# Fifteen copies of x issued on SyncE instead of GpSimd, and a conditional block in place of a zero-or-one loop

## The chip, the core and the metric

One NeuronCore of a Trainium2 chip runs the whole program. The metric is the device time of one execution in microseconds, as the median of several. All engine times below come from one profiled execution; a line such as L678 is line 678 of the kernel before.

## What is computed

Two transformer blocks for one sequence of 512 tokens of width 1024, in float32. The first has an SSD (Mamba-2) mixer beside a forgetting attention of 16 heads, and a convolution-gated MLP. The second has retention, sliding-window attention, a two-level mixture of 32 experts with two experts for each token, and a gated per-layer embedding. What the change touches:

```python
# first block, forgetting attention (x itself is not needed for it)
logits = einsum(qh, kh) * scale + cum[..., None] - cum[:, :, None, :]
# second block, experts: top-1 group, then top-2 experts inside it
combine = sum(one_hot(expert_id) * (g_w * top_p)[..., None])
for grp in range(4):
    hid = silu(einsum('td,edf->tef', hf, w_gate[sl])) * einsum('td,edf->tef', hf, w_up[sl])
    y = y + einsum('tef,efd->td', hid * combine[:, sl, None], w_down[sl])
x = x + y
x = x + sigmoid(rms_norm(x, ple_gate_norm_g) @ w_ple_gate) * ple
```

## The kernel before, in words

Each float32 product is made of three passes over a high and a low part (`mm3`, L251 to L253), so TensorE carries nearly the whole program. Weights come in chunks of 128x1024 through `fetch` (L217), which issues a 512 KB transfer on SyncE into a `wr` tile; ScalarE makes the high part `wh` (L205) and VectorE or GpSimd the low part `wl` (L208). In the first block there are two `wr` tiles and three pairs of `wh` and `wl`, so a transfer waits for a free `wr`, and a split for a free pair.

The stages follow one another: load x and the constants and normalise x (L361 to L363) tile by tile, with `n_mix`, one row of weights spread over all partitions (L351); the projection z (L416); the gates and their sums, written to the DRAM tile `sums` (L476); the SSD mixer in two groups (L480 to L582), which reads `sums` back into `ab` (L546); the forgetting attention for four groups of heads, two pairs of heads each, which reads `sums` back into `ncum` (L680); and then the other stages up to the experts and the closing gate with the output (`gated`, L1858 to L1861).

`ydram` is a DRAM tile of 30 x 64 rows of 1024 for the rows that the experts give. Before any expert writes to it, it is filled with rows of x: fifteen copies of 128 rows, 512 KB each, from DRAM to DRAM, so that rows that no expert writes hold finite numbers. They stand in the attention's loop in the code (L677, L678) and are issued by GpSimd. The experts' results are scattered into `ydram` by GpSimd near the end of the program (L1540) and gathered from it (L1796).

`overflow` (L1149) handles tokens beyond the 64 slots of an expert. Every engine loads two registers, `rounds` and `some` (L1157, L1159). `some` is 0 or 1, and the work stands in a loop over range(0, some) (L1161). In these inputs no expert has more than 64 tokens, so the body is not executed: the trace holds no instruction of it.

Nothing here but the stretches under `manual_schedule` has its order written by hand: the framework's list scheduler orders each engine's instructions, and puts an instruction with no open dependency as early as its queue allows. `tc.issue_after(ins)` adds an edge of issue order alone: what is traced inside the block on the engine of `ins` comes behind `ins` in that engine's queue. SyncE's queue is in order, and its transfers take turns on eight semaphores, so that a transfer also waits for the one eight places earlier to land.

Of the kernel before, what the change touches and what calls it, by code (L numbers as in the profile page):

```python
# [19 lines left out]
T = 512  # L20
# [384 lines left out]
def first_mixer(c, xt, zraws):  # L405

    tc, nc, a = c.tc, c.nc, c.a
# [58 lines left out]
    sums = c.dram.tile([2, 16, T], F32, name="sums")  # L466
# [123 lines left out]
    with tc.tile_pool(name="fox", bufs=1) as p:  # L590
        offs = [0, 128, 384, 768]

        def scores(qs, kd, kl, ncum):

            pb = p.tile([128, 1280], F32, name=c.name("pb"), tag="pb", bufs=2)
            den = c.sm([128, NT], tag="den")
            rden = c.sm([128, NT], tag="rden")
            for t in range(NT):
                n = 128 * (t + 1)
                tb = slice(t * 128, t * 128 + 128)  # L600
                sc = c.aux()
                pe.matmul(sc[:, :n], qs[:, tb], kd[:, :n], start=True, stop=False)
                pe.matmul(sc[:, :n], qs[:, tb], kl[:, :n], start=False, stop=False)
                pe.matmul(sc[:, tb], c.identb, c.upneg, start=False, stop=True)


                ns = p.tile([128, T], F32, name=c.name("ns"), tag="ns", bufs=3)
                nm = c.sm([128, 1], tag="nm", bufs=4)
                v.tensor_tensor_reduce(ns[:, :n], sc[:, :n], ncum[:, :n], scale=-1.0, scalar=3e38,
                                       op0=OP.add, op1=OP.min, accum_out=nm)  # L610
                pt_ = pb[:, offs[t]:offs[t] + n]
                s.activation(pt_, ns[:, :n], AF.Exp, scale=-1.0, bias=nm, accum_out=den[:, t:t + 1])
                v.reciprocal(rden[:, t:t + 1], den[:, t:t + 1])
                v.tensor_scalar(pt_, pt_, rden[:, t:t + 1], None, op0=OP.mult)
            return pb

        def values(pb, vv, out):

            po = c.aux()
            ptile = [p.tile([128, 1280], F32R, name=c.name("pT"), tag=f"pT{k}", bufs=2) for k in range(2)]  # L620
            pos = 0
            for js in ((0,), (1,), (2, 3)):
                pt = c.aux()
                o, spans = 0, []
                for j in js:
                    st = o
                    for t in range(j, NT):
                        c.transpose(pt[:, o:o + 128], pb[:, offs[t] + j * 128:offs[t] + j * 128 + 128])
                        o += 128
                    spans.append((j, pos + st, o - st))  # L630
                c.split(ptile[0][:, pos:pos + o], ptile[1][:, pos:pos + o], pt[:, :o])
                pos += o
                for j, st, n in spans:
                    for k in range(2):
                        pe.matmul(po[:, j * 128:], vv[:, j].rearrange("p x d -> p (x d)"),  # L635
                                  ptile[k][:, st:st + n], start=j == 0 and k == 0, stop=j == NT - 1 and k == 1)
            tmp = p.tile([64, T], F32, name=c.name("ot"), tag="ot", bufs=1)
            s.activation(tmp, po[64:128], AF.Copy)
            v.tensor_tensor(out, po[0:64], tmp, op=OP.add)


        kls = [[p.tile([128, T], F32R, name=c.name("kl")) for _ in range(n)] for n in (1, 2)]
        for i in range(2):
            for kl in kls[i]:
                v.memset(kl[64 - 64 * i:128 - 64 * i].bitcast(F32), 0.0)
        pending = []

        c.ydram = c.dram.tile([COMBINED * SLOTS, D], F32, name="ydram")
        blocks = [(i, a["x"][i % T:i % T + 128]) for i in range(0, COMBINED * SLOTS, 128)]
        for hg in range(4):  # L650
            qk = []
            for i in range(2):
                r = fin.tile([128, NT, 4, 64], F32, name=c.name("qk"), tag=f"qk{i}", bufs=2)
                ss = c.sm([128, NT, 4], tag="qss")

                def eat(tp, ps):
                    ps4 = ps.rearrange("p t (h d) -> p t h d", h=4)
                    sq = fin.tile([128, 2, 4, 64], F32, name=c.name("sq"), tag="sq", bufs=1)
                    s.activation(sq, ps4, AF.Square)
                    s.activation(r[:, 2 * tp:2 * tp + 2], ps4, AF.Copy)  # L660
                    v.tensor_reduce(ss[:, 2 * tp:2 * tp + 2], sq, axis=AX.X, op=OP.add)

                c.proj_b(xt, a["wqkv"][hg, i], eat)
                rs = c.rsqrt(ss.rearrange("p t h -> p (t h)"), 1.0 / 64, "qr")
                r3 = r.rearrange("p t h d -> p (t h) d")
                v.tensor_tensor(r3, r3, rs[:, :, None].to_broadcast([128, 16, 64]), op=OP.mult)
                qk.append(r)
            vv = fin.tile([128, NT, 4, 2, 64], F32R, name=c.name("v"), tag="v", bufs=2)

            def eat_v(tp, ps):  # L670
                ps4 = ps.rearrange("p t (h d) -> p t h d", h=4)
                t2 = slice(2 * tp, 2 * tp + 2)
                c.split(vv[:, t2, :, 0], vv[:, t2, :, 1], ps4)

            c.proj_b(xt, a["wqkv"][hg, 2], eat_v)
            for pr in range(2):
                for i, rows in blocks[4 * hg + 2 * pr:4 * hg + 2 * pr + 2]:  # L677
                    nc.gpsimd.dma_start(c.ydram[i:i + 128], rows)  # L678
                ncum = fin.tile([128, 2, T], F32, name=c.name("ncum"), tag="ncum", bufs=2)
                nc.sync.dma_start(ncum, sums[1, 4 * hg + 2 * pr:4 * hg + 2 * pr + 2][None].to_broadcast([128, 2, T]))  # L680
                pq, pk = c.aux(), c.aux()
                for ps, src in ((pq, qk[0]), (pk, qk[1])):
                    for t in range(NT):
                        c.transpose(ps[:, t * 128:t * 128 + 128],
                                    src[:, t, 2 * pr:2 * pr + 2].rearrange("p h d -> p (h d)"))

                qs = [p.tile([128, T], F32R, name=c.name("qs"), tag=f"qs{i}", bufs=2) for i in range(2)]
                kd = [p.tile([128, T], F32R, name=c.name("kd"), tag=f"kd{i}", bufs=2) for i in range(2)]
                kl = [k[pr % len(k)] for k in kls]
                kn = c.col("kn")  # L690
                for i in range(2):
                    hi, lo = slice(64 * i, 64 * i + 64), slice(64 - 64 * i, 128 - 64 * i)
                    s.activation(qs[i][hi], pq[hi], AF.Copy, scale=qn[hi])
                    v.scalar_tensor_tensor(qs[i][lo], pq[hi], qn[hi], qs[i][hi].bitcast(F32), op0=OP.mult, op1=OP.subtract)
                    s.activation(kd[i][hi], pk[hi], AF.Copy, scale=kn[hi])
                    s.activation(kd[i][lo], pk[hi], AF.Copy, scale=kn[hi])
                    v.scalar_tensor_tensor(kl[i][hi], pk[hi], kn[hi], kd[i][hi].bitcast(F32), op0=OP.mult, op1=OP.subtract)
                for i in range(2):
                    pb = scores(qs[i], kd[i], kl[i], ncum[:, i])
                    pending.append((pb, vv[:, :, 2 * pr + i], mixf[64 * i:64 * i + 64, 2 * hg + pr, :]))  # L700
                    if len(pending) > 1:
                        values(*pending.pop(0))
        for x in pending:
            values(*x)
# [444 lines left out]
def overflow(c, x, routing, slot, wt, extra, pled, out):  # L1149
# [3 lines left out]
    tc, nc, a = c.tc, c.nc, c.a  # L1153
# [4 lines left out]
                            skip_runtime_bounds_check_because="the count of tokens bounds it")  # L1158
    some = nc.values_load(extra[0:1, 1:2], min_val=0, max_val=1, skip_runtime_bounds_check_because="0 or 1")  # L1159
    wgu, wdn = a["wgu"].rearrange("e p c -> (e p) c"), a["wdn"].rearrange("e p c -> (e p) c")  # L1160
    with tc.For_i(0, some, 1):  # L1161
        ring = c.more_ring(2, 5)
        p = tc.alloc_tile_pool(name="over", bufs=1)
        rel = p.tile([128, 2, NT], F32, name="rel")
# [293 lines left out]
def experts(c, x, routing, xtp, pled, out):  # L1458
# [342 lines left out]
    for pool in (ring4, p, p0, ring3, op):  # L1801
        pool.release()
    routing.ring.release()
    overflow(c, x, routing, slot, wt, extra, pled, out)
    moe.release()

# [57 lines left out]
def emit(tc, a, out, dbg=None, stop=None):  # L1864
    with ExitStack() as ctx:
# [15 lines left out]
        for t in range(NT):  # L1881
            xn = c.sm([128, D], tag="xn", bufs=2, pool=x0)
            c.normalize(xin[t], w, xn, xn)
            c.to_xt(xn, _block(xt, t))
        x0.release()
        mixs, mixf, xpool, mixf_pool = first_mixer(c, xt, raws)
        xt = _xt_tiles(c, xtp, "xt")
        for t in range(NT):
# [43 lines left out]
```

## Time and profile before

| | |
|---|---|
| median of 3 runs (lowest to highest) | 1603.81 us (1602.76 to 1604.42) |
| the profiled execution: its own time | 1600.57 us |
| the profiled execution: span from the first to the last instruction | 1598.8 us |
| outside the span, in the profiled execution | 1.77 us |
| TensorE busy | 1517.5 us, 95% of the span |
| copies into ydram (L678) | 15 of 512 KB, 9.9 / 12.9 / 15.5 us from issue to landing (least / median / most) |

How to read it: the span is what the trace covers. PE is TensorE, PEld its weight loads, DVE VectorE, ACT ScalarE, POOL GpSimd, SP SyncE; a "q" behind a name (SPq, POOLq) marks what the engine's sequencer does alone, such as issuing a transfer, a wait or a branch. q0 is the queue of GpSimd's transfers, q1 that of SyncE's.

### The profile page before, as it was taken

To read this page: it belongs to the slowest core of one execution; us is meant where nothing else is said; L and a number is where in the kernel's file an instruction comes from. 1 tells how busy PE (TensorE), PEld (TensorE's weight loads), DVE (VectorE), ACT (ScalarE), POOL (GpSimd) and SP (SyncE) were. 2 spreads that over 40 slices of the span, in tenths; PEclk is the share of its full clock that TensorE was granted. 3 is DMA by queue.
4 is the path that set the end of the run, shared out by engine and by line. 5 is a ranking of instruction groups with operands and counts; after the bars stand their busy time and mean duration, and the time that the engine had idled before them with its cause. 6 is when DMAs were issued, how large, how long until landed. Compare 5 with 4: busy or idle time off the path is not lost.

```text
span 1598.8 us, 24250 instructions
## 1 busy us (share of the span) xinstructions
PE 1517.5 (95%) x9603; PEld 1254.7 (78%) x9603; DVE 898.8 (56%) x1980; ACT 663.1 (41%) x1103; POOL 111.2 (7%) x102
## 2 busy tenths in 40 slices
PE   4997999999999999999999999899999999999987
PEld 3776888998899988998889998787888864554456
DVE  4378778778874766336653523868654453223165
ACT  3364747567742544224442333569612421111133
POOL 3043310000000000000000000300000001000020
PEclk9998999999999999999999999999999999999999
DMA  9342222222341533233332433221323699999971
GB/s 321 94 157 80 66 67 80 93 79 68 106 145 41 169 96 98 74 106 106 97 92 90 163 105 102 93 93 48 98 66 126 242 338 410 409 410 410 402 275 56
DMA packets 75944, 246.62 MB, mean 154 GB/s; under 512 B 9486, under 2 KB 18446, under 8 KB 75456
## 3 DMA queue, kind: packets, MB, share of 16 engines
q1 hardware_dynamic: 69152, 220.80, 39.6%
q0 software_dynamic: 4944, 17.91, 3.0%
q10 hardware_dynamic: 1728, 6.29, 1.0%
q8 instruction: 78, 1.28, 0.3%
q14 instruction: 42, 0.34, 0.1%
HBM read 234.86 MB, written 24.18 MB: 162 GB/s over the span
## 4 chain that ended last, share of the span: by engine, by line
PE 74%; DVE 12%; ACT 6%; DMA 5%; issue 2%; POOL 0%; SPq 0%; ACTq 0%; DVEq 0%; POOLq 0%
PE acc L252 18%; PE acc L251 18%; PE acc L253 18%; PE acc L1117 5%; PE aux L355 3%; PE aux L1485 3%; PE acc L1137 3%; DMA wc<-in_wgu_dram 2%; DVE wl L208 1%; PE aux L635 1%; ACT wh L205 1%; DMA wr<-in_wz_dram 1%; PE aux L522 1%; DMA wc<-in_wpleg_dram 1%; DMA wc<-in_wdn_dram 1%
## 5 line engine op out<-in xcount | busy, mean ns | idle before, releaser
L208 DVE TENSOR_TENSOR wl<-wr,wh 128x1024 fp32r<-128x1024 f32 (+1 forms) x177 | 213.7, 1210 | 266.0 <-ACT wh L205 260.9
L205 ACT ACTIVATE wh<-wr 128x1024 fp32r<-128x1024 f32 (+1 forms) x181 | 188.4, 1046 | 328.7 <-PE acc L253 166.9
L253 PE MATMUL acc<-xth,wl 128*128 128x512 f32 (+2 forms) x744 | 278.1, 374 | 0.1
L252 PE MATMUL acc<-xtl,wh 128*128 128x512 f32 (+2 forms) x744 | 277.9, 374 | 0.0
L251 PE MATMUL acc<-xth,wh 128*128 128x512 f32 (+2 forms) x744 | 277.8, 373 | 0.1
L251 PE MATMUL acc<-wh,xth 128*128 128x256 f32 x912 | 257.3, 283 | 4.4 <-ACT xth L205 2.2
L252 PE MATMUL acc<-wl,xth 128*128 128x256 f32 x912 | 256.8, 282 | 2.1 <-DVE wl L208 2.1
L253 PE MATMUL acc<-wh,xtl 128*128 128x256 f32 x912 | 256.8, 283 | 0.8 <-DVE xtl L208 0.8
L251 PEld LDWEIGHTS acc<-wh,xth 128*128 128x128 f32 x912 | 172.1, 189 | 7.1 <-ACT xth L205 2.8
L252 PEld LDWEIGHTS acc<-wl,xth 128*128 128x128 f32 x912 | 172.2, 189 | 4.5 <-DVE wl L208 3.4
L253 PEld LDWEIGHTS acc<-wh,xtl 128*128 128x128 f32 x912 | 172.1, 189 | 1.6 <-DVE xtl L208 1.0
L251 PEld LDWEIGHTS acc<-xth,wh 128*128 128x128 f32 (+1 forms) x744 | 139.6, 188 | 26.4 <-issue 0.8
L253 PEld LDWEIGHTS acc<-xth,wl 128*128 128x128 f32 (+1 forms) x744 | 139.6, 188 | 26.0 <-issue 0.8
L252 PEld LDWEIGHTS acc<-xtl,wh 128*128 128x128 f32 (+1 forms) x744 | 139.5, 188 | 23.8 <-issue 0.2
L1117 PE MATMUL acc<-wc,xg 128*64 128x512 f32 x512 | 115.5, 593 | 0.4 <-DMA wc<-in_wgu_dram 0.4
L251 PE MATMUL acc<-wh,acth 128*128 128x256 f32 x352 | 99.0, 281 | 0.1
L252 PE MATMUL acc<-wl,acth 128*128 128x256 f32 x352 | 98.2, 279 | 0.0
L253 PE MATMUL acc<-wh,actl 128*128 128x256 f32 x352 | 98.0, 279 | 0.0
L1117 PEld LDWEIGHTS acc<-wc,xg 128*64 128x64 f32 x512 | 37.4, 137 | 74.9 <-issue 63.3
L251 PEld LDWEIGHTS acc<-wh,acth 128*128 128x128 f32 x352 | 66.5, 189 | 0.6 <-ACT acth L205 0.6
L252 PEld LDWEIGHTS acc<-wl,acth 128*128 128x128 f32 x352 | 66.6, 189 | 0.1
L774 DVE SCALAR_TENSOR_TENSOR fcv<-acc,cols,fcv 128x511 f32<-128x511 f32 x88 | 65.7, 747 | 1.5
(464 smaller groups left out, 2555.6 us busy)
## 6 DMA issues: line engine op xcount, KB each, us to landing
wc<-in_wgu_dram SPq DMA_DIRECT2D x128, 512.0 KB
wc<-in_wdn_dram SPq DMA_DIRECT2D x64, 512.0 KB
wr<-in_wup_dram SPq DMA_DIRECT2D x44, 512.0 KB
wr<-in_w2a_dram SPq DMA_DIRECT2D x28, 512.0 KB
wr<-in_wqkv_dram SPq DMA_DIRECT2D x24, 512.0 KB
wr<-in_wout_dram SPq DMA_DIRECT2D x24, 512.0 KB
wr<-in_wdown_dram SPq DMA_DIRECT2D x16, 512.0 KB
ydram<-in_x_dram POOLq DMA_DIRECT2D x15, 512.0 KB, 12.9
```

Source lines behind the costliest of these rows:

```text
L205: nc.scalar.activation(hi, src, AF.Copy)
L208: (nc.vector if engines[1] == "v" else nc.gpsimd).tensor_tensor(lo, src, hi.bitcast(F32), op=OP.subtract)
L251: mm(out, a[0], b[0], start=start, stop=False)
L252: mm(out, a[0], b[1], start=False, stop=False)
L253: mm(out, a[1], b[0], start=False, stop=stop)
L355: self.nc.tensor.transpose(out, src, self.ident[:rows, :rows])
L522: pe.matmul(py[:, h * 64:h * 64 + 64], de[:, h], xd[:, h], start=True, stop=True)
L635: pe.matmul(po[:, j * 128:], vv[:, j].rearrange("p x d -> p (x d)"), ptile[k][:, st:st + n], start=j == 0 and k == 0, stop=j == NT - 1 and ...
L774: v.scalar_tensor_tensor(y[:, sh:], ps[:, :T - sh], cv(k), y[:, sh:], op0=OP.mult, op1=OP.add)
L1117: c.nc.tensor.matmul(ps[self.half(i)], xg(kb, i), self.wu[kb // 2][i][:, kb % 2 * 512:kb % 2 * 512 + 512], start=kb == 0, stop=kb == KB - 1)
L1137: c.nc.tensor.matmul(ps[n][self.half(i)], self.hT[:, j, self.half(i)], self.wd[j][i][:, n * 512:n * 512 + 512], start=j == 0, stop=j == 1)
L1485: pe.matmul(ps[:, j], hf[t][:, k, ks], oq[:, t], start=start and k == 0, stop=stop and k == 1)
```

## The change

Two edits. In the attention's loop the copies move from GpSimd to SyncE, each two of them behind the transfer of `ncum` of the same pair of heads. In `overflow` the loop over range(0, some) becomes a conditional block with the label "more", and ahead of it, behind the closing gate in the code, a location for a branch hint of that label is marked with "LikelyTaken". The body of the block is the same.

```diff
             for pr in range(2):
-                for i, rows in blocks[4 * hg + 2 * pr:4 * hg + 2 * pr + 2]:
-                    nc.gpsimd.dma_start(c.ydram[i:i + 128], rows)
                 ncum = fin.tile([128, 2, T], F32, name=c.name("ncum"), tag="ncum", bufs=2)
-                nc.sync.dma_start(ncum, sums[1, 4 * hg + 2 * pr:4 * hg + 2 * pr + 2][None].to_broadcast([128, 2, T]))
+                sent = nc.sync.dma_start(ncum, sums[1, 4 * hg + 2 * pr:4 * hg + 2 * pr + 2][None].to_broadcast([128, 2, T]))
+                with tc.issue_after(sent.ins):
+                    for i, rows in blocks[4 * hg + 2 * pr:4 * hg + 2 * pr + 2]:
+                        nc.sync.dma_start(c.ydram[i:i + 128], rows)
                 pq, pk = c.aux(), c.aux()
...
     wgu, wdn = a["wgu"].rearrange("e p c -> (e p) c"), a["wdn"].rearrange("e p c -> (e p) c")
-    with tc.For_i(0, some, 1):
+    tc.mark_branch_hint_location("more", "LikelyTaken")
+    with tc.If(some > 0, label="more"):
         ring = c.more_ring(2, 5)
```

## Rows read from the trace of the kernel before

**Rows 1.** The page: busy time of each engine, share, instructions.
```profile
PE 1517.5 (95%) x9603; PEld 1254.7 (78%) x9603; DVE 898.8 (56%) x1980; ACT 663.1 (41%) x1103; POOL 111.2 (7%) x102
```

**Rows 2.** Stretches: length, busy time by engine, clock, DMA share, GB/s.
```profile
0.00:20.00 20.00, 2.27 (x9) 1.86 (x9) 2.82 (x9) 4.16 (x7) 4.66 (x13) 1.00 0.90 316
20.00:40.00 20.00, 13.81 (x101) 13.03 (x101) 13.94 (x33) 11.10 (x18) 8.90 (x14) 1.00 0.95 328
80.00:100.00 20.00, 19.74 (x94) 15.92 (x93) 17.11 (x37) 17.14 (x24) 3.66 (x3) 1.00 0.77 259
100.00:110.00 10.00, 8.73 (x38) 6.21 (x37) 4.71 (x8) 8.26 (x11) 6.23 (x5) 1.00 0.01 2
280.00:320.00 40.00, 39.62 (x324) 37.55 (x325) 31.87 (x84) 23.57 (x48) 0.00 (x0) 1.00 0.29 93
```

**Rows 3.** Time order of the start on POOL, DVE, ACT, PE: start, length, what.
```profile
1.38 1.69 POOL L678 DMA_DIRECT2D ydram<-in_x_dram  x3 [0.82 <-POOLq L1924]
6.03 1.45 POOL L678 DMA_DIRECT2D ydram<-in_x_dram  x3
24.00 3.97 POOL L678 DMA_DIRECT2D ydram<-in_x_dram  x8
...
4.58 1.06 ACT L361 ACTIVATE xn<-xin 128x1024 f32<-128x1024 f32 x1 [2.45 <-DMA xin<-in_x_dram]
14.40 1.28 DVE L363 SCALAR_TENSOR_TENSOR xn<-xin,rsy,n_mix 128x1024 f32<-128x1024 f32 x1 [7.21 <-DMA n_mix<-in_rows_dram]
...
19.92 1.06 ACT L205 ACTIVATE wh<-wr 128x1024 fp32r<-128x1024 f32 x1 [0.27 <-DMA wr<-in_wz_dram]
21.36 1.05 ACT L361 ACTIVATE xn<-xin 128x1024 f32<-128x1024 f32 x1
...
30.18 0.36 PE L251 MATMUL acc<-wh,xth 128*128 128x256 f32 x1
```

**Rows 4.** Queues from 2.5 to 15 us: packets, MB, share of 16 engines.
```profile
q0 software_dynamic: 169, 3.01, 65.9%
q1 hardware_dynamic: 469, 1.59, 37.5%
```

**Rows 5.** All queues together from 17.5 to 22.5 us.
```profile
DMA packets 627, 1.99 MB, mean 399 GB/s; under 512 B 121, under 2 KB 154, under 8 KB 627
```

**Rows 6.** Queues from 25 to 42.5 us, same columns.
```profile
q0 software_dynamic: 282, 4.69, 74.9%
```

**Rows 7.** The SSD stage: SP's issues, one split, one DVE step.
```profile
81.00 3.71 SPq L680 DMA_DIRECT2D ncum<-sums  x2
86.26 5.08 SPq L217 DMA_DIRECT2D wr<-in_wxbc_dram  x2
91.47 4.15 SPq L546 DMA_DIRECT2D ab<-sums  x2
...
105.88 1.05 ACT L205 ACTIVATE wh<-wr 128x1024 fp32r<-128x1024 f32 x1
...
101.89 0.99 DVE L549 TENSOR_TENSOR ssde<-ab,acs 128x8 f32<-128x8 f32 x1 [2.84 <-POOL xe L568]
```

**Rows 8.** The attention: SP's issues, and the split that follows.
```profile
280.27 0.33 SPq L680 DMA_DIRECT2D ncum<-sums  x1
284.19 9.97 SPq L217 DMA_DIRECT2D wr<-in_wqkv_dram  x3
...
291.22 1.06 ACT L205 ACTIVATE wh<-wr 128x1024 fp32r<-128x1024 f32 x1
```

**Rows 9.** The end: last output, L1161 and L1928; ns least/median/most, first, last start.
```profile
1591.28 0.33 SPq L1861 DMA_DIRECT2D out_dram<-g  x1
...
L1161 PEldq COMPARE_BRANCH  x2: 197/1907/3617, 1590.0 to 1595.0; - x2
L1161 POOLq COMPARE_BRANCH  x1: 33/33/33, 1594.0 to 1594.0; - x1
...
L1928 POOLq DRAIN  x3: 46/103/3832, 1594.2 to 1598.6; - x3
```

## The prediction

> **What bounds the kernel now.** The page comes first: TensorE is busy for 95% of the span, GpSimd for 7% [rows 1]. So a change can gain only where TensorE is idle, and a load on another engine or queue costs only where TensorE comes to wait for it. I therefore read the stretches next [rows 2]. TensorE works 2.27 of the first 20 us and 13.81 of the next 20, and 39.62 of 40 in the attention: 23.9 us are idle in the first 40, and hardly any where the copies stand in the code. Third, the start in order of time [rows 3]: GpSimd issues six copies by 7.5 us and eight more from 24 us. VectorE, whose statistics of the first tile are ready at 7.2 us (14.40 less its wait of 7.21), waits for `n_mix` until 14.40; ScalarE splits the second chunk of wz at 19.92 and only then turns to the second tile of x at 21.36; TensorE's unbroken run begins at 30.18. Fourth, the queues. From 2.5 to 15 us q0, where the copies are, moved 3.01 MB and q1, where the loads are that all wait for, 1.59 [rows 4]. From 17.5 to 22.5 us, with next to nothing on q0, the rate was 399 GB/s [rows 5]. The start is therefore bound by loads that share the DMA engines with copies which nothing needs before the experts scatter.
>
> **The change part by part.** *Removed: the copies at the start.* GpSimd's issue time (15 x 0.5 us) matters little: GpSimd waits for ScalarE anyhow. What counts is what q1 could have done. SyncE issues, by the code and with the sizes that follow from it, x0, the constants (384 KB), `n_mix`, wz0, cols (132), rows (54), wz1, then x1 to x3, each other one of 512 KB. x0 has landed at 4.58, where ScalarE starts on it [rows 3]. Behind it, `n_mix` is 896 KB away, 0.917 MB, and at 399 GB/s lands at 4.58 + 2.3 = 6.9. VectorE then starts at 7.2, bound by its own statistics, instead of 14.40: 7.2 us earlier. wz1 is 2106 KB behind x0, 2.157 MB, 5.4 us: 10.0. wz0 is 3.6 us behind, 8.2. ScalarE goes on in its present order: wz0 from 8.2, the first half of the transposed tile from about 9.7 (VectorE's 1.28 us from 7.2, then four transposes), wz1 from 10.3, the second half from 11.3, and the second tile of x from 11.9 instead of 21.36. x1 needs 1.3 us more than wz1, 11.3, and is there. That is 9.5 us earlier, and everything up to 30.18 hangs on it: the transposes of tiles 1 and 2 stand in TensorE's queue ahead of that run. The bounds: at 328 GB/s, the rate of the second 20 us with both queues at work [rows 2], wz1 lands at 11.2 and the gain is 8.3; and if the planner, with its loads early, puts the first products ahead of the transposes, the run could begin two passes of VectorE over a chunk (1.28 us each, as at L363) behind wz1's split at 11.3, at 13.9: a gain of 16. I take **9.5**, as the present order is the nearest row. The run after 30.18 waits for products and splits of its own, so that the shift is kept.
>
> *Added: the same copies on SyncE.* Between 25 and 42.5 us q0 moved 4.69 MB, 8.9 copies, in 74.9% of 17.5 us: 1.46 us for a copy on all 16 engines [rows 6]. The first two `ncum` are issued far ahead of the attention, from 81 us, in the SSD stage [rows 7]; four copies land behind them there, 5.9 us of DMA time, and SyncE's issue of each is some 0.3 to 0.4 us. Queued behind them on SyncE are two chunks of wxbc and two `ab`. The first chunk is issued at 86.26 and split at 105.88, 19.6 us later, so 5.9 us is hidden. `ab` has less room: the DMA engines work at 77% up to 100 us and stand still (1%) from 100 to 110 [rows 2], so the backlog ends near 106 instead of 100, while VectorE takes the first of these `ab` at 101.89, behind GpSimd [rows 7]. The cost lies between nothing (GpSimd covers it) and 5.9 us (all of it on the path); by order of issue that `ab` lands before the last one, so I take **1.5**. The other eleven copies go behind the six later `ncum`, in the attention. The one at 280.27 is of the tighter kind, of which there are three: a chunk follows at 284.19 and is split at 291.22, 7 us later [rows 8], against 2.9 us for two copies that began 3.9 us before. This costs nothing: the 7 us in which the chunk waits for its split hide it, and without them it would be 2.9 us for a group. The scatter comes with the experts, long after the last copy.
>
> *The conditional block.* The branch that passes the body over stalls TensorE's sequencer for 3617 ns from 1590.0, but what ends last is GpSimd: its branch at 1594.0, then a DRAIN of 3832 ns from 1594.2, and the final barrier behind it [rows 9]. TensorE is through at 1595.2, the end of its last branch, so its stall is covered by GpSimd's DRAIN, some 2.8 us to spare. GpSimd's branch waits for every queue, the last output among them (issued at 1591.28); I see nothing in the edit that removes that or the DRAIN. Bounds: a gain of 3.8 if the DRAIN can run before the last output lands, a loss of 3.6 if another engine on the path comes to stall as TensorE does. I take **0**, what the order of the rows gives.
>
> Sum: -9.5 + 1.5 + 0 = -8.0. Against the profiled execution, 1598.8 of span and 1.77 outside, that is 1592.6; this execution lies 3.2 us below the median of the runs, from which the forecast is **1595.8**.
>
> [...] GpSimd's DRAIN follows a branch, as TensorE's 3617 ns lie on one [rows 9]. [...]
>
> **The rivals.**
> *More is won.* GpSimd's 3.8 us leave the path, because its DRAIN can run early or is a wait like TensorE's 3617 ns that the mark saves: -8.0 - 3.8 gives 1592.0. Or the planner reorders the start for the full 16: 1595.8 - 6.5 = 1589.3. For it: the end is a chain of waits with no work in it. Against: the DRAIN stands behind a wait for all queues.
> *It is taken back.* The start gives its lower 8.3, and the whole backlog of 5.9 us falls on the path: 2.4 less than before, 1601.4. For it: VectorE reaches for `ab` within 2 us of the backlog's present end. Against: GpSimd is what it waits for there.
> *Copies ahead of weights.* The copies take on SyncE what they took on GpSimd from issue to landing, 12.9 us in the median, one after another. The four in the SSD stage then take 51.6 us against 18.3 of room (19.6 less 1.3 for the chunk itself): a loss of 33. In the attention a pair takes 25.8 against 9.6 (3.9 and 7.0, less 1.3): 16 us for each of the two full groups of the tighter kind. 33 + 32 - 9.5 = 56 slower, 1660. It decides from (18.3 + 9.5) / 4 = 7 us for a copy. Against: 1.46 us measured when the engines worked on them.
> *The edit does not do what it says*, and the copies stay at the start: they stand behind `ncum`, whose first transfer is at 81 us, so this has no chance of its own.
>
> **How the numbers follow.** The forecast (1592.5 to 1599) has 0.58; the further gain (below 1592.5) 0.18; a gain partly lost (1599 to 1600.6) 0.08; taken back (within 0.2%, 3.2 us, about what a measurement of this kernel can tell from no change) 0.11; copies ahead of weights 0.05. So faster 0.84, same 0.11, slower 0.05. The range, 1588.5 to 1601, leaves out the top part of the fourth case, the last, and a little of the second.
>
> **What would show it.** Right: no L678 on GpSimd; `n_mix` awaited until about 7 us, not 14.40; TensorE's run from about 20.7; copies on SyncE behind `ncum`, four of them in the SSD stage; splits of wqkv still waiting for products and not for DMA; GpSimd's DRAIN of 3.8 us still last. Wrong: VectorE waiting for `ab` by several us, ScalarE's splits released by wr transfers, a run that begins after 23 us, a different order of the SSD stage, or a span that ends without that DRAIN.

## The result and the profile after

| | before | after |
|---|---|---|
| median of five runs each | 1603.67 us | 1587.25 us (1581.83 to 1589.20) |
| ratio, 95% interval | | 0.9894 [0.9875, 0.9914] |
| the profiled execution: its own time, its span | 1600.57, 1598.8 | 1589.17, 1587.3 |

Faster by 16.4 us in the medians and by 11.5 in the span of the two profiled executions. The forecast was 1595.8 with a range down to 1588.5: the direction is right, the gain too small, and the median lies 1.25 us below the range. The median of before over the 60 runs made in all is 1602.0, and of the 11 runs of the program of after (five here, six in the fifth experiment, which runs the same instructions) 1587.7: a gain of 14.3. From here on, a line such as L1163 is that of the kernel whose trace is shown; *the end* is the time from the issue of the last output to the end of the span.

The start first. Busy time of TensorE, weight loads, VectorE, ScalarE and GpSimd in two stretches, then the granted clock, DMA share and GB/s; [rows 2] has the same two of before:

```profile
0.00:20.00 20.00, 9.05 (x42) 7.42 (x42) 8.86 (x26) 11.21 (x17) 6.07 (x11) 1.00 0.79 265
20.00:40.00 20.00, 18.96 (x159) 18.33 (x160) 8.99 (x18) 6.89 (x14) 0.00 (x0) 1.00 0.18 60
```

TensorE works 28.0 of the first 40 us where it worked 16.1. The timeline of DVE, ACT and PE, to be laid beside [rows 3]:

```profile
7.38 1.28 DVE L363 SCALAR_TENSOR_TENSOR xn<-xin,rsy,n_mix 128x1024 f32<-128x1024 f32 x1 [0.34 <-DMA n_mix<-in_rows_dram]
...
8.99 1.06 ACT L205 ACTIVATE wh<-wr 128x1024 fp32r<-128x1024 f32 x1 [3.41 <-DMA wr<-in_wz_dram]
...
11.93 1.06 ACT L205 ACTIVATE wh<-wr 128x1024 fp32r<-128x1024 f32 x1 [0.56 <-DMA wr<-in_wz_dram]
...
13.37 1.05 ACT L361 ACTIVATE xn<-xin 128x1024 f32<-128x1024 f32 x1
...
11.42 0.58 PE L251 MATMUL acc<-wh,xth 128*128 128x256 f32 x1 [0.73 <-ACT xth L205]
...
12.91 0.41 PE L253 MATMUL acc<-wh,xtl 128*128 128x256 f32 x1
13.13 0.41 PE L251 MATMUL acc<-wh,xth 128*128 128x256 f32 x1
...
16.98 0.28 PE L251 MATMUL acc<-wh,xth 128*128 128x256 f32 x1
17.09 0.28 PE L252 MATMUL acc<-wl,xth 128*128 128x256 f32 x1
...
17.68 1.09 PE L355 MATMUL aux<-cst,xn 128*128 128x128 f32 x8 [0.20 <-DVE rsm L326]
```

VectorE's wait for `n_mix` is over at 7.38 us instead of 14.40, ScalarE splits the second chunk of wz at 11.93 instead of 19.92 and reaches the second tile of x at 13.37 instead of 21.36. So far the forecast holds, if up to 1.6 us late. But TensorE does not stand waiting for that tile any more: the products of tile 0 run from 11.42 on, *ahead of* the transposes of the second tile at 17.68. The scheduler has put them into another order.

The queues, packets and rate, from 2.5 to 15 us, and packets of all queues with their sizes from 4.4 to 12 us, the stretch in which the second chunk of wz comes in:

```profile
q1 hardware_dynamic: 1452, 4.32, 100.6%
...
DMA packets 914, 2.42 MB, mean 318 GB/s; under 512 B 231, under 2 KB 359, under 8 KB 914
```

The same line of before from 17.5 to 20 us, a part of [rows 5]:

```profile
DMA packets 355, 1.01 MB, mean 404 GB/s; under 512 B 89, under 2 KB 122, under 8 KB 355
```

The loads have the DMA engines to themselves (4.32 MB against 1.59 in [rows 4]), but at 318 GB/s, not at the 399 of [rows 5]. Small packets alone don't explain that: a quarter of them are under 512 B here (231 of 914), and a quarter in the 2.5 us of before that went at 404 (89 of 355). What slows this stretch, in which `n_mix`, `cols` and `rows` come, is not shown.

The SSD stage, SyncE's issues:

```profile
62.36 3.84 SPq L476 DMA_DIRECT2D sums<-sumrow  x2
...
69.00 3.97 SPq L678 DMA_DIRECT2D ncum<-sums  x1
73.02 0.61 SPq L681 DMA_DIRECT2D ydram<-in_x_dram  x1
80.34 0.58 SPq L681 DMA_DIRECT2D ydram<-in_x_dram  x1
84.11 0.57 SPq L678 DMA_DIRECT2D ncum<-sums  x1
84.73 2.76 SPq L681 DMA_DIRECT2D ydram<-in_x_dram  x2
...
251.38 0.33 SPq L678 DMA_DIRECT2D ncum<-sums  x1
```

`sums` is written from 62.36 us, in before from 74.33: the start is worth 12.0. The third `ncum` goes out at 251.38, in before at 261.01: 9.6, so 2.4 are lost between. The next stretch loses nothing (the chunk of wqkv behind two copies is issued at 274.58, in before at 284.19 [rows 8], again 9.6), the rest of the program 0.4 (last output 1582.07 against 1591.28 [rows 9]).

The end: the last output, then the branch (L1163) and the closing barrier (L1930) by engine, with ns least/median/most, first and last start:

```profile
1582.07 0.33 SPq L1863 DMA_DIRECT2D out_dram<-g  x1
...
L1163 POOLq COMPARE_BRANCH  x1: 45/45/45, 1514.3 to 1514.3; - x1
...
L1163 PEldq COMPARE_BRANCH  x1: 4005/4005/4005, 1579.5 to 1579.5; - x1
...
L1930 POOLq DRAIN  x3: 40/107/2609, 1531.2 to 1585.5; - x3
...
L1930 ACTq DRAIN  x2: 8/8/8, 1582.2 to 1585.2; - x2
...
L1930 PEldq DRAIN  x2: 8/8/8, 1583.7 to 1587.1; - x2
```

From the last output's issue to the end: 5.2 us, in before 7.5. GpSimd is through the branch at 1514.3, and its long DRAIN, 2.61 us, starts at 1531.2, some 50 us before the end. The branch still costs TensorE 4.0 us, and now TensorE is last: its second DRAIN (an instruction of the closing barrier) starts at 1587.1, those of the others at 1585.2. In sum -12.0 + 2.4 + 0.4 - 2.3 = -11.5, the span.

### The profile page after: what moved, and what is told of

Read it like the earlier page. It is cut to its first block, busy times and chain, and to the rows that moved or that the text cites. A ratio compares the mean times of both kernels' runs of the same rounds, so it can differ in the third digit from the quotient of the medians.

```text
span 1587.3 us, 24178 instructions
## 1 busy us (share of the span) xinstructions
PE 1521.1 (96%) x9603; PEld 1257.0 (79%) x9603; DVE 896.4 (56%) x1980; ACT 662.9 (42%) x1103; POOL 103.6 (7%) x87
## 4 chain that ended last, share of the span: by engine, by line
PE 78%; DVE 11%; ACT 6%; issue 3%; DMA 2%; POOL 0%; SPq 0%; ACTq 0%; POOLq 0%; DVEq 0%
PE acc L251 18%; PE acc L252 18%; PE acc L253 18%; PE acc L1118 6%; PE aux L355 4%; PE aux L1487 3%; PE acc L1138 3%; DVE wl L208 1%; PE aux L635 1%; ACT wh L205 1%; PE aux L522 1%; DVE de L555 1%; ACT pb L612 1%; DMA wc<-in_wgu_dram 1%; DVE xn L363 1%
```

## The experiments

Each was run beside the kernel before on the same chip; the ratio is that of its time to the time of before, with its 95% interval. Stretches and ends are those of one profiled execution each. *The SSD stretch* is the time from the first write of `sums` to the issue of the third `ncum`.

**1. Copies moved, loop kept** (from the kernel after):

```diff
-    tc.mark_branch_hint_location("more", "LikelyTaken")
-    with tc.If(some > 0, label="more"):
+    with tc.For_i(0, some, 1):
```

> The copies on SyncE as in the kernel after, with the loop of the kernel before. Theory (two gains that add: about 9.6 us from the start less the SSD stage's give-back, about 2.3 us from the end): the writes of sums from 62.4 us, the first ncum of the attention from 251.4, and from the issue of the last output to the end of the span the 7.5 us of the kernel before, with GpSimd's DRAIN of 3.8 us last; time about 9.5 us below the kernel before, 2 above the kernel after. Rival (the end of before was only late by chance, the conditional block does nothing): the last output to the end 5.2 us here too, and the time of the kernel after.

Measured 1587.63 us, ratio 0.9905 [0.9875, 0.9935]: nearly all of the gain is the copies', and in the time nothing of the block can be seen (after 1587.25). `sums` from 62.85, the third `ncum` at 249.24, last output 1579.62, span 1586.0: 6.4 us of end, neither the 7.5 nor the 5.2 expected. GpSimd's DRAIN is last again, but it takes 2612 ns instead of 3832 [rows 9]: 1.1 us of the end come with the copies' leaving GpSimd. And the four copies are in the SSD stage here too, yet the SSD stretch is 186.4 us, as in before (186.7), not 189.0.

**2. Conditional block and mark, copies on GpSimd as before.**

> The copies on GpSimd at the start as before, with the conditional block and the mark. Theory: sums written from 74.3 us as before, GpSimd through its branch tens of us before the end, its DRAIN off the path, and 5.2 us in place of 7.5 from the issue of the last output to the end: 2.3 us faster. Rival: the block saves the whole DRAIN of 3.8 us. Second rival: no difference, as GpSimd passes the branch early only when it has no copies of its own.

Measured 1599.63 us, ratio 0.9985 [0.9967, 1.0003]: 2.1 us faster than the 1601.73 of before beside it, which the interval does not quite tell from nothing. So the gain of the block rests on the traces. There the theory holds: `sums` from 75.46 (1.1 later than in before, with the same copies at the start), GpSimd's branch at 1527.2, the last output issued at 1593.14 and the span 1598.2, so 5.1 us of end, 2.4 less than before. The barrier's rows say what took the DRAIN's place:

```profile
L1929 POOLq DRAIN  x3: 46/103/3829, 1543.4 to 1598.0; - x3
L1929 SPq DRAIN  x3: 7/7/7, 1595.9 to 1597.7; - x3
...
L1929 PEldq DRAIN  x2: 8/8/8, 1597.4 to 1597.8; - x2
```

The DRAIN of 3829 ns is gone from the path whole, but TensorE, through its branch by 1594.1, comes to its first DRAIN only at 1597.4, 1.5 us behind SyncE's. The second rival falls: GpSimd passes early with copies of its own too. The first is right that the whole DRAIN leaves the path, but TensorE takes back 1.5 us of it.

**3. The order on TensorE.** The kernel after, with the first products behind the transposes of the first three tiles (`turned2` is the last of these):

```diff
-    z = project_z(0)
+    with tc.issue_after(c.turned2.ins):
+        z = project_z(0)
```

> The kernel after, but TensorE's first products stand behind the transposes of the first three tiles, as in the kernel before. Theory (about 8 us of the start come from earlier loads, 4 from the order that the scheduler now finds): n_mix awaited until 7.4 us as in the kernel after, the unbroken run from about 21, sums written from about 66 us: 4 us slower than the kernel after. Rival (the loads alone give all 12): sums from 62.4 us, the same time as the kernel after.

Measured 1592.48 us, ratio 0.9926 [0.9898, 0.9953]. TensorE's and SyncE's timeline:

```profile
8.84 1.97 PE L355 MATMUL aux<-cst,xn 128*128 128x128 f32 x8 [8.84 <-DVE xn L363]
18.32 1.97 PE L355 MATMUL aux<-cst,xn 128*128 128x128 f32 x8 [7.52 <-DVE rsm L326]
21.08 1.94 PE L355 MATMUL aux<-cst,xn 128*128 128x128 f32 x8 [0.79 <-DVE xn L363]
22.67 0.56 PE L251 MATMUL acc<-wh,xth 128*128 128x256 f32 x1
...
23.24 0.41 PE L253 MATMUL acc<-wh,xtl 128*128 128x256 f32 x1
23.46 0.41 PE L251 MATMUL acc<-wh,xth 128*128 128x256 f32 x1
...
67.78 3.84 SPq L477 DMA_DIRECT2D sums<-sumrow  x2
```

This is the start that the prediction worked out, nearly in the order of before (there three products already stood ahead of the third tile): 22.67 for the run (forecast 20.7), which is 7.5 us earlier than 30.18, and `sums` 6.5 us earlier. The 1.0 between is TensorE's: from the run's start to `sums` it is busy for 44.3 us, in before for 43.3, and the first products of this run start 0.21 us apart. So of the 12.0 us the earlier loads give 6.5 and the order 5.4, much as the theory had it (8 and 4). In 7.52 us of idle time ahead of 18.32 one sees what the order fills.

**4. Only six copies at the start.** The kernel before with the block; of the copies on GpSimd the first six stay, nine stand behind GpSimd's last work in the SSD stage.

> The kernel before with the conditional block, but of the fifteen copies on GpSimd only the first six stand at the start, and nine stand behind GpSimd's last work of the SSD stage. Theory (what costs is the copies that run beside n_mix and wz, before 17 us): n_mix awaited until 14.4 us, the second chunk of wz split at 19 to 20, sums from 72 to 74.3 us, so at most 2 us of the 12 come back. Rival (each copy counts alike, also the eight from 24 us on): 9/15 of 12, sums from about 67 us.

Measured 1604.61 us, ratio 1.001 [0.999, 1.003]. `n_mix` is awaited until 14.94, `sums` written from 75.89: with six copies the start is as late as with fifteen. So the theory holds there, and 9/15 of the 12 us did not come. But the nine are issued together at 235.8 us, and ScalarE then waits 6.5 us for a chunk of wqkv, in an SSD stretch of 194.1 us instead of 186.7. Of these 7.4 us 2.7 are idle time of TensorE (22.0 us against 19.3); in the other 4.7 it is busy longer, with 22.2 us of its work at half clock against 10.9 (see under 7). Nine at once on GpSimd's queue do hold up a chunk; their price is some 2.7 us, and whether the clock is part of it is open.

**5. Without the mark.**

```diff
-    tc.mark_branch_hint_location("more", "LikelyTaken")
```

> The kernel after without the line that marks a location for the branch hint. Theory (the mark does nothing): TensorE's stall at the branch stays at 3.5 to 4 us, the last output's issue to the end 5.2 us, the time that of the kernel after. This run is also a second look at the SSD stage of the same program: if the 2.4 us that the kernel after lost there were a lower granted clock and not the four copies, the stretch from the writes of sums to the third ncum, 186.7 us before and 189.0 after, can come out anywhere between, with TensorE's busy time moving with it. Rival (the mark is what shortens the end): the end grows back towards 7.5 us, 2 us slower than the kernel after. Rival (the copies cost 2.4 us in the SSD stage): the stretch is 189.0 again.

Measured 1588.48 us, ratio 0.9907 [0.9888, 0.9926]. The traces hold 24178 instructions with the mark and without, and no hint among them: given without an engine, the mark leaves none in the program. TensorE's branch takes 3.4 us, the end 4.5. So 0.7 us of the end lies between two executions of one program. The SSD stretch is 189.1 again, which is what the second rival said; the first experiment, with the same four copies there and 186.4, speaks against it, and so do the numbers under 7.

**6. No copy in the SSD stage**, three behind each `ncum` from the third on:

```diff
+                n = 2 * hg + pr - 2
                 with tc.issue_after(sent.ins):
-                    for i, rows in blocks[4 * hg + 2 * pr:4 * hg + 2 * pr + 2]:
+                    for i, rows in (blocks[3 * n:3 * n + 3] if n >= 0 else ()):
```

> The kernel after with no copy in the SSD stage: three copies behind each ncum from the third on, none behind the first two. Theory (the four copies in the SSD stage cost nothing): the stretch from the writes of sums to the third ncum about 186.5 us, as in the run with the loop (186.4), and the time that of the kernel after. Rival (they cost the 1.5 us that was forecast, or 2.4): the kernel after less 1.5 to 2.4 us. Three copies at a time in the attention take 4.4 us of the DMA engines against 7 us of room: nothing by either.

Measured 1584.71 us, ratio 0.9890 [0.9871, 0.9909]; the SSD stretch 186.3, `sums` from 62.34, the end 3.6 us. The stretch is as the theory had it; the time, 2.5 us below after, is what the rival said. But the two profiled executions lie 5.0 us apart, of which 2.8 are the stretch and 1.6 the end; and with four copies in it the stretch was 186.4 as well, in the first experiment. All five runs are below 1585.5 us, where five of the six of the fifth, on the same chip, are above; the tenth, with the copies in the same places, did not repeat that.

**7. All fifteen in the SSD stage**, behind the first `ncum` (`for i, rows in () if hg + pr else blocks`):

> The kernel after with all fifteen copies behind the first ncum, so that they go in the SSD stage, where before there were four; 22 us of DMA time by 1.46 us a copy. Theory (a chunk issued behind copies waits for their transfer, and the room is 19.6 us for the first chunk of wxbc and some 2 us for ab): ScalarE or VectorE waits for wxbc, ab or wz there, 5 to 15 us slower than the kernel after. Rival (the copies run in time that nobody needs, at any number): no difference. Rival (each costs its time from issue to landing, as copies ahead of weights): 60 us or more.

Measured 1586.48 us, ratio 0.9901 [0.9878, 0.9924]; the stretch 187.6, the end 3.7. ScalarE waits 3.3 us for a chunk of wxbc there, but 2.7 without any copy (experiment 6). The scheduler spread the copies from 73 to 119 us between the chunks; so spread, the rival "at any number" holds to about 1 us. The SSD stretch of all runs but the fourth, with TensorE's busy time in it, the part of that which fell where the granted clock was 0.50 (*at half clock*), and TensorE's idle time:

| kernel | copies in it | us | TensorE busy | of it at half clock | idle |
|---|---|---|---|---|---|
| before | 0 | 186.7 | 167.4 | 10.9 | 19.3 |
| experiment 2 | 0 | 187.0 | 167.2 | 11.5 | 19.8 |
| experiment 6 | 0 | 186.3 | 166.7 | 9.7 | 19.6 |
| experiment 9 | 0 | 189.7 | 173.4 | 23.6 | 16.3 |
| experiment 10 | 0 | 189.9 | 170.3 | 17.1 | 19.5 |
| experiment 11 | 0 | 187.5 | 167.6 | 11.0 | 20.0 |
| experiment 1 | 4 | 186.4 | 166.7 | 10.0 | 19.7 |
| experiment 3 | 4 | 187.6 | 167.6 | 11.1 | 20.0 |
| after, experiments 5 and 8 | 4 | 189.0, 189.1, 188.8 | 169.6, 169.7, 169.8 | 15.9, 15.4, 15.7 | 19.4, 19.4, 19.1 |
| experiment 7 | 15 | 187.6 | 167.2 | 11.1 | 20.4 |

The time does not go with the copies. The busy time goes with how much of TensorE's work falls into windows at half clock: less half of that part it is 161.4 to 162.1 us in every row. What is left for the copies to cost is idle time: 19.1 to 20.0 us with four copies, 19.3 to 20.0 with none outside experiment 9, 20.4 with fifteen. The windows of after and of experiment 6, columns as above (the second number is TensorE's busy time):

```profile
115.49:125.73 10.24, 9.02 (x29) 6.79 (x30) 4.54 (x9) 3.18 (x4) 2.08 (x2) 0.50 0.35 101
139.38:146.21 6.83, 6.83 (x26) 5.70 (x26) 4.28 (x7) 1.88 (x2) 0.93 (x1) 0.50 0.24 79
62.36:251.38 189.02, 169.57 (x1055) 144.83 (x1053) 139.20 (x309) 105.33 (x156) 54.51 (x38) 0.95 0.33 101
```

```profile
116.01:119.43 3.42, 2.86 (x8) 2.00 (x9) 1.62 (x3) 1.72 (x2) 1.04 (x1) 0.50 0.83 214
136.49:143.32 6.83, 6.79 (x25) 5.76 (x26) 4.19 (x7) 1.88 (x2) 1.04 (x1) 0.50 0.25 79
62.34:248.60 186.26, 166.70 (x1055) 142.67 (x1053) 139.10 (x309) 105.36 (x156) 54.60 (x38) 0.97 0.30 91
```

The same 1055 matmuls take TensorE 2.9 us longer in after, and the stretch is 2.8 longer. In after 15.9 us of them ran at half clock, in experiment 6 9.7; half of the difference is 3.1.

**8. A hint that is in the program.** The kernel after; the hint names TensorE and stands behind products, 48 matmuls ahead of the branch; the old mark is left out:

```diff
+        with c.tc.issue_after(c.lastmm.ins):
+            c.tc.mark_branch_hint_location("more", "LikelyTaken", engines=[mybir.EngineType.PE])
         for o in (0, 256):
```

> The kernel after with the hint given for TensorE and placed in its queue behind the products before the last two groups (48 matmuls of 256 columns ahead of the branch). Theory (TensorE's stall at the branch is code that has not arrived, and its late DRAIN in the final barrier is the next piece of code): the stall falls from 4.0 us to under 0.5, TensorE's DRAIN in the barrier comes with the others, and the last output's issue to the end falls from 5.2 to about 3.6 us. Rival (the hint points at the other arm, or too early): stall and end as in the kernel after.

Measured 1586.00 us, ratio 0.9902 [0.9883, 0.9921]. Last output and closing, as above for after:

```profile
1579.42 0.33 SPq L1865 DMA_DIRECT2D out_dram<-g  x1
...
L1163 PEldq COMPARE_BRANCH  x1: 499/499/499, 1576.9 to 1576.9; - x1
...
L1932 PEldq DRAIN  x2: 8/8/8, 1578.2 to 1582.6; - x2
...
L1932 ACTq DRAIN  x2: 8/8/8, 1581.6 to 1582.5; - x2
...
L1932 PEldq BRANCH_PREFETCH_HINT  x1: 45/45/45, 1567.9 to 1567.9; - x1
```

The stall falls from 4005 to 499 ns, TensorE's last DRAIN comes with the others, and 3.6 to 3.7 us are left from the last output to the end. A hint 9 us earlier takes 3.5 us away. In the stall of after, 1579.5 to 1583.5, the trace has one packet of 0.02 MB on q8, whose kind is instruction, from 1580.6 us, and another from 1584.2, ahead of the DRAIN at 1587.1. That fits the theory; that TensorE waits for these packets is not shown. But the stall alone is not what the end waits for: experiments 6 and 7 end in 3.6 and 3.7 us with a branch of 3.4 and 3.5. What makes the difference is the late DRAIN behind it. Of the nine profiled executions with the block and no hint, seven end in 4.5 to 5.4 us; in after and experiments 2 and 4, which are among them, TensorE's DRAIN comes 1.9, 1.5 and 1.7 us behind SyncE's, and in experiment 6 together with it (both at 1581.8). The two with the hint, here and experiment 10, end in 3.7 and 3.6 us. That the hint is the reason is not shown by two executions.

**9. Copies on SyncE, right behind the load of the last tile of x** (`issue_after` that load, not `ncum`):

> The kernel after, but the copies stand on SyncE right behind the load of the last tile of x: the scheduler puts four ahead of wdtf, six ahead of the first chunk of wxbc, four and one between later chunks; the order on TensorE, VectorE, ScalarE and GpSimd is that of the kernel after. Theory (a copy costs only where it runs beside n_mix and the first two chunks of wz, and behind them in SyncE's order it can't): n_mix awaited until 7.4 us, second chunk of wz split at 12, sums written from 62.4 to 65 us, at most 3 us slower than the kernel after. Rival (any copy in the first 60 us takes the loads' bandwidth): 22 us of DMA time ahead of the chunks, sums from 70 us or later, 8 us slower or more.

Measured 1585.16 us, ratio 0.9903 [0.9885, 0.9921]. SyncE's issues:

```profile
12.56 3.18 SPq L217 DMA_DIRECT2D wr<-in_wz_dram  x2
15.79 2.49 SPq L681 DMA_DIRECT2D ydram<-in_x_dram  x4
24.35 0.34 SPq L217 DMA_DIRECT2D wr<-in_wdtf_dram  x1
24.73 3.65 SPq L681 DMA_DIRECT2D ydram<-in_x_dram  x6
...
35.23 2.49 SPq L681 DMA_DIRECT2D ydram<-in_x_dram  x4
...
46.49 0.49 SPq L681 DMA_DIRECT2D ydram<-in_x_dram  x1
...
62.29 3.84 SPq L476 DMA_DIRECT2D sums<-sumrow  x2
```

All copies are issued by 47 us, and `sums` is written as early as in after. The theory holds: the copies need not leave the start; they must only not run beside `n_mix` and the first two chunks of wz. (The profiled execution, at 1593.09 the slowest of the five, lost it again later: the SSD stretch took 189.7 us with no copy in it, and the end 5.4.)

**10. Late copies and the hint together** (experiments 6 and 8):

> No copy in the SSD stage (three behind each ncum from the third on) and the hint in TensorE's queue. Theory: the start of the kernel after (sums from 62.4 us), the SSD stretch 186.3 us if the granted clock falls there for no longer than without copies, the branch 0.5 us and the last output's issue to the end 3.65 us: 3 to 4 us faster than the kernel after, ratio to the kernel before about 0.988. Rival (each of the two gains was a chance of one run): the time of the kernel after.

Measured 1587.83 us, ratio 0.9912 [0.9895, 0.9929]: no faster than after. `sums` from 62.37, the end 3.6 us, both as the theory had them; but the SSD stretch, without a copy, was 189.9 us, with 17.1 us of TensorE's work at half clock. In time the rival was right. Nothing that was tried beats the kernel after by more than the runs' spread.

**11. All copies on GpSimd, from 15 us on**, behind its second low part of wz:

> All fifteen copies on GpSimd's queue as before, but behind GpSimd's second low part of wz, so from some 13 us on, and with the conditional block. The scheduler finds TensorE's order of the kernel after. Theory (the moment counts, not the queue): n_mix awaited until 7.4 us, second chunk of wz split at 12, the copies run from 13 to 36 us beside the next two chunks of wz, which may come some us later: sums written at 62.4 to 66 us, and a time within 4 us of the kernel after. Rival (GpSimd's queue is what hurts, it takes two thirds of the bandwidth wherever it stands): sums from 70 us, most of the gain gone.

Measured 1591.82 us, ratio 0.9937 [0.9916, 0.9958]. `n_mix` until 7.53, the second chunk of wz split at 11.94, the order of after on TensorE; but `sums` from 66.71, 4.3 us later than in after, and the split of wdtf, TensorE behind it and a window of the granted clock say why:

```profile
38.24 0.42 ACT L205 ACTIVATE wh<-wr 128x256 fp32r<-128x256 f32 x1 [4.10 <-DMA wr<-in_wdtf_dram]
...
38.98 0.39 PE L251 MATMUL acc<-wh,xth 128*128 128x256 f32 x1 [2.75 <-ACT z L416]
...
40.37:43.78 3.41, 3.41 (x19) 3.41 (x18) 0.00 (x0) 0.38 (x1) 0.00 (x0) 0.50 0.88 322
```

Each of theory and rival is half right: the moment is worth 7.6 us of the 12.0. Of the other 4.3, 2.8 are idle time of TensorE, the wait for wdtf (in after it is split at 34.02, without a wait); in 1.6 TensorE is busy longer, at half clock for 3.4 us, where after and experiment 9 have no such window before `sums`. Whether the copies brought that on is not shown. In experiment 9 the copies begin at nearly the same time (15.8 us against 15.4), but in one queue with the loads and between them, spread to 47 us where GpSimd is done by 33, and cost nothing. ScalarE waits 4.1 us for wdtf with the copies on GpSimd and not at all with them on SyncE. Queue and spread changed together, so that the 2.8 us can't be split between them.

## Why the prediction was right or wrong

The forecast was 8.5 us too high. The start gave 2.5 more than forecast and the end 2.3, the SSD stage took 0.9 more and the rest of the program 0.4: 3.5 us by these rounded terms. The other 5.1 come from the step from the profile to the median.

**The start: right in its mechanism, wrong in its size (-9.5; measured -12.0).** That the copies beside the first loads made the start late is shown by experiments 4 (six copies there are enough to keep it late) and 9 (fifteen just behind the loads cost nothing). Two errors of opposite sign lie in the number. The rate: the prediction took 399 GB/s, measured on other loads, for a stretch that ran at 318; why it was slower is not shown. The second chunk of wz was split at 11.93 and the second tile begun at 13.37, forecast 10.3 and 11.9. In the present order, experiment 3, the tile began at 14.05 and the run 7.5 us earlier than in before, less than even the lower bound of 8.3; and of that 6.5 arrived at `sums`, so that "the shift is kept" failed by 1.0 as well. And the order: "I take 9.5, as the present order is the nearest row" is the step that failed. The prediction named the other order, priced it at 16 in all and put it among the rivals; it came, and is worth 5.4. The framework's scheduler does not keep an order when the loads move: with its loads early it had work for TensorE in the 7.5 us in which the present order has it wait.

**The SSD stage (+1.5; +2.4 in the profiled pair, nothing by the copies).** That the number is near is luck. Four copies cost nothing that the runs can show (experiment 1 against 6: 186.4 and 186.3), fifteen about 1 us; VectorE's wait for `ab`, which the term was to price, is 0.4 us in after. Of the 2.4 that after loses there 2.2 are busy time of TensorE, with 15.9 us of its work at half clock against 10.9. The bound of nothing held; the 1.5 was a choice between the bounds.

**The attention (0): right.** The chunk behind two copies goes out 9.6 us earlier, as does the `ncum` ahead of it, and ScalarE's splits of wqkv still wait for products.

**The conditional block (0; measured -2.3).** The step that failed is the reading "GpSimd's branch waits for every queue", of which it says "I see nothing in the edit that removes that or the DRAIN". The wait belongs to the loop: in experiment 1 all engines pass three branches each and meet ahead of the last one, which GpSimd takes at 1582.4, and its DRAIN of 2.61 us comes behind that, from 1582.6. The block has one branch and no such meeting, in after SyncE alone waits for the last output (its first DRAIN at 1584.9, 2.8 us behind the issue), and GpSimd goes through 68 us before it is issued. A span that ends without that DRAIN was one of the prediction's own signs of being wrong. So the rival "GpSimd's 3.8 us leave the path" was right in what leaves, but not by the mark that the prediction held possible for it: the mark is not in the program. 3.9 and 3.8 us are gained in experiments 6 and 7 (7.5 to 3.6 and 3.7), 2.1 to 3.0 in after and the six others; TensorE comes to its DRAINs in time in experiment 6 and late in after and experiments 2 and 4. Without the block the copies' leaving alone shortens the DRAIN from 3.83 to 2.61 us and the end by 1.1 (experiment 1); with the block it is off the path at 3.83 us (experiment 2) as at 2.61 (after). In the median times the block's gain is not clear of noise (experiments 1 and 2).

**From the profile to the median (+3.2).** The forecast's profiled time, 1592.6, was 3.4 us too high against 1589.17. The other 5.1 of the miss are the step that took before's offset for after's, the largest single error: before's profiled execution lay 3.2 below the median of three runs, but 1.5 below that of 60, and after's lay 1.9 above that of its five. Executions of one program spread by 7 us and more here (after 1581.83 to 1589.20), and three of them don't give an offset to a microsecond.

**Copies ahead of weights.** It did not happen in after, and experiment 7 puts its price at next to nothing where the scheduler spreads the copies. Nine at once, in experiment 4, made one chunk wait 6.5 us, but they stood on GpSimd's queue and not ahead of it on SyncE.

What stays open: why the first window at half clock lasts 3.4 us in experiment 6, 6.8 in before and 10.2 in after, and why the tenth experiment has a third one in the SSD stretch, where it does the same work as the sixth. What the new order on TensorE would give with the copies still at the start was not tried.

## What to carry to other kernels

Ask of a transfer that nothing needs soon what it runs beside: here fifteen copies beside the loads that open the kernel made the start 12.0 us later, and right behind those loads, in their own queue, they cost nothing (experiment 9), so that they need not go far away. Before a few microseconds in a long stretch are put down to an edit, look how much of TensorE's work ran at half clock on either side. When an edit moves loads, ask what order the scheduler will find with them, because that can be worth as much as the loads. At the end of a program look for what each engine does alone, which one comes late to its DRAINs (here TensorE, by 1.9 us) and what makes all engines wait for one, and read from the trace whether a hint is in the program at all.

## What the runs showed of the hardware

GpSimd's long DRAIN takes 3.83 us in before and in experiments 2 and 4, with copies on GpSimd, and 2.61 in after and in experiments 1, 6 and 8, with none there. TensorE's branch over the unused body takes 3.4 to 4.0 us (before 3.62, after 4.01, experiments 1, 2 and 6 3.39, 3.48 and 3.44) and 0.50 with a hint issued 9 us ahead of it (experiment 8). In after TensorE is late once more behind the branch, for one of its DRAINs, by 1.9 us (1585.2 to 1587.1); what it waits for there is not shown. In after TensorE's products of 256 columns start 0.21 us apart at 13 us and 0.11 apart at 17 us, though the granted clock of that stretch reads 1.00, and in experiment 3 they start 0.21 apart at 23 us and 0.11 at 26. So in both the first products ran at half the pace of the later ones; why is not shown.
